# Attention's output projection: the first pair of blocks by seven block products on half of its rows, and a fixed order for the last four heads

## The chip, the cores and the metric

The kernel runs on one core of a Trainium2 chip. The metric is the device time of one launch in microseconds (us), the median of several runs. Five engines work side by side, each through its own list of instructions in order, and wait for one another by semaphores: TensorE (PE, matrix products, with its weight loads PEld), VectorE (DVE), ScalarE (ACT), GpSimd (POOL) and SyncE (SP); here SP issues nearly all loads of weights, and POOL issues loads that add into a tile that is there already.

## The reference, cut to what matters

Two decoder layers over 256 positions of width 2048. Layer 0 has recurrent mixers, layer 1 attention with 16 heads of 128; both are followed by a squared-ReLU MLP of width 8192. The part that the change touches is the end of layer 1's attention and the matrix products behind it:

```python
def dilated_attention(h, positions, w_qkv, w_o):
    qkv = (h @ w_qkv).astype(F32).reshape(bsz, seq, 3, ATTN_HEADS, HEAD_DIM)
    q = partial_rope(qkv[:, :, 0], positions) * (HEAD_DIM ** -0.5)
    k = partial_rope(qkv[:, :, 1], positions)
    v = qkv[:, :, 2]
    ...
    out = (num / den).reshape(bsz, seq, D_MODEL).astype(h.dtype)
    return out @ w_o

def squared_relu_mlp(h, w1, w2):
    return jnp.square(jax.nn.relu(h @ w1)) @ w2
...
        h = h + mix
        h = h + squared_relu_mlp(rms_norm(h, norm_mlp[layer]), mlp_w1[layer], mlp_w2[layer])
```

## The kernel before

**Precision.** Every large product is made from two-part operands: a value is split into `hi` (rounded to the format that PE takes, fp32r) and `lo` (the rest), for weights and activations alike. A product takes three passes: hi x hi, lo x hi and hi x lo. For weights, `Weights.split` (L104, L105) makes the parts: ACT casts `hi`, DVE subtracts to get `lo`. A weight tile ("slab") is 128 x 2048 float32, 1 MB, and is four sub-blocks of 128 x 512. Activations lie in `bufa` (what the projections and w1 read) and `bufb` (what w_o and w2 read): 16 blocks of 128 features, of 256 positions each, hi and lo side by side. In attention, block hd of `bufb` is the output of head hd.

**The stream of weights.** `units` lists all slabs in the order of use. `unit()` hands out the next one and, when few are left ahead, calls `fetch()`, which loads and splits another. So a split's place in the program is set by the slab that PE has begun, two to four slabs earlier, and the Tile framework's scheduler places it among the other instructions of ACT and DVE by priorities (`stream`, `urgent`). `after` and `add_manual_dep` fix an order within one engine.

**Seven products for eight.** For w1, w2 and the value part of w_qkv, the first half of the rows is taken as 2 x 2 blocks: even and odd feature blocks by two output blocks (512 columns each) of the weights, and the two halves of the positions by even and odd feature blocks of the activations. A scheme with seven products of such blocks takes the place of the usual eight. `blocks` runs it. The steps are called a, t1, t2, c, d, t3, t4, besides the plain slabs n (n2, n3, n6, n7), which have 24 matmuls each against 12 for a product step. Weights are combined on the way: s = a + t1 on DVE, the slab c is added to t1 by a load on POOL's queue, then s = s + c on DVE (L134), and a last slab is added to s by another load on POOL's queue. Activations are combined into `formh` and `formx` (`combos`, `part_forms`). Each sum lives in a PSUM bank: beta takes a, t2 and t3 in turn, alpha takes t1 and c. A bank has to be read before the next step writes it; in `second` (the w2 blocks) `to_x` does that, by adding the bank into the residual `xall`/`xres` on DVE (L769). ORDERS gives the order of the steps: for w2 and w_qkv a, t1, n7, t2, c, n6, t3, d, n2, t4, n3. `combine` (L128 to L160) holds the loads and additions of a step. For all but w1 it orders the addition s = s + c behind the split of the slab fetched at that time (`after(i, [made[u].last])`).

**The end of attention.** For each head `scores` projects q (16 + 16 matmuls, `project`), normalises and rotates it (`normed`, `rope`: L431 to L436, L869 to L872 on DVE), does the same for k, multiplies q by k on PE (L882, L883), adds the mask table (L885), takes the maximum (L889), exponentials with a running sum on ACT (L224), a reciprocal and a scaling (L891, L893), transposes the three blocks on PE (L896) and copies them out on ACT (L898). `mix` multiplies the values by these weights (L904, L905) and splits the result into `bufb` (L251 on ACT, L252 on DVE). Heads 12 to 15 run as `mix(12 + i, scores(40 + 2 * i), vg)`. Matmuls that go through `mm` or `turn` are kept in program order on PE by `chain`; those through `T.matmul` and `T.transpose` are placed by the scheduler.

**The output projection.** `out_project` takes w_o plainly, for each of four output blocks four slabs by `tokens`, `add_res` adds the sums to the residual (L624), and `to_features` transposes the result, splits it into `bufa` and, for the first two blocks, makes `formx`. The host lays w_o out beforehand, as it does the other weights. `PAIRED` is the order of feature blocks that the scheme of seven products wants, which brings the halves of the rows next to each other.

Of the kernel before, what the change touches and what calls it, by code (L numbers as in the profile page):

```python
# [41 lines left out]
def trunk_kernel(ctx, tc, x, xtok, cols, tab, masks, pos, fin, w_in, w_gate, w_out, w_qkv, w_o, w1, w2, out):  # L42
# [22 lines left out]
    units = []  # L65
    made = {}

    def plan(src, n):
        units.extend((src, i) for i in range(n))

    def plan2(src, i):
        for what, u in ORDERS[src is not w1]:
# [8 lines left out]
    for layer in range(2):  # L81
        if layer:
            for v, heads in ((0, 24), (32, 8)):
                plan2(w_qkv, v)
                units.extend((w_qkv, v + 8 + i) for i in range(heads))
            plan(w_o, 16)
        for q in range(4):
            for src in (w1, w2):
                for n in range(0, 4, 2):
                    plan2(src, layer * 64 + q * 16 + 4 * n)  # L90
    at = [0, 0]

    class Weights:
# [7 lines left out]
        def split(self, at, n):  # L101
            h, l = self.part(at, n)
            w = self.raw[:, at:at + n]
            A.copy(h, w)  # L104
            i = V.tensor_tensor(l, w, h.bitcast(F32), OP.subtract)  # L105
            self.ins = getattr(i, "ins", i)
            self.last = self.ins.name

        def part(self, at, n):
            return self.hi[:, at:at + n], self.lo[:, at:at + n]  # L110
# [12 lines left out]
            nc.sync.dma_start(r, src[i])  # L123
            made[u] = Weights(r, 1024)

    held, waiting, read = {}, [], []

    def combine(u, src, i, what, i0):  # L128
        def load(name, j, home=wraw):
            held[name] = home.tile([P, 2048], F32, name="raw" if home is wraw else name)  # L130
            nc.sync.dma_start(held[name], src[j])

        def add(to, x, y):
            return V.tensor_tensor(held[to], held[x], held[y], OP.add)  # L134
# [12 lines left out]
        if ahead == ("t2",):  # L147
            load("c", i0 + 5)
            nc.gpsimd.dma_start(held["t1"], src[i0 + 5], accum_op=OP.add)
            if src is not w1:  # L150
                make()
            i = add("s", "s", "c")
            if src is not w1:
                after(i, [made[u].last])
        if src is w1 or ahead != ("t2",):
            make(2048 if src is w1 or what != "t2" else 0)
        if src is not w1 and what == "t2":
            waiting.append(made[u])
        if what == "c":
            nc.gpsimd.dma_start(held["s"], src[i0 + 1], accum_op=OP.add)  # L160

# [33 lines left out]
    def turn(out_, in_):  # L195
        chain[:] = [after(T.transpose(out_, in_, ident), chain)]  # L196

    later, turns = [], []

    def flush(due=None):  # L200
        todo = later[:due]
# [139 lines left out]
            V.scalar_tensor_tensor(r, t, 1.5, r, op0=OP.add, op1=OP.mult)  # L341

    def tokens(src, i0, mov, kgs=(0, 1, 2, 3), by_k=False):
        ks = range(KB)
        ps = [pmm.tile([P, 512], F32, name="p") for _ in range(2)]
        for g in kgs:
            w = unit(src, i0 + g)
            order = [(j, i) for i in range(4) for j in range(2)] if by_k else \
                [(j, i) for j in range(2) for i in range(4)]
            for j, i in order:  # L350
                k = ks[4 * g + i]
                h, l = w.part(i * 512, 512)
# [297 lines left out]
    def out_project(src, gname, kgs):  # L650
        nrm = Norm()
        for n in range(4):
# [6 lines left out]
    def blocks(src, i0, n0, mov, forms, events, final):  # L659
# [21 lines left out]
        for what, u in ORDERS[src is not w1]:  # L681
            w = unit(src, None if u is None else i0 + 4 * n0 + u)
            due = len(later)
            if what != "n":
                times(bank[what], w, side[what])
                if what in events:
                    events[what](bank[what])
                if what == "t1" and waiting:
                    with stream():
                        w = waiting.pop()  # L690
                        w.split(0, 2048)
                        tc.add_manual_dep(w.ins, read[-1], NOSYNC, reason="order on one engine")
            else:
                n, g = divmod(u, 4)
                plains[n] += 1
                for j in (1, 0) if n else (0, 1):
                    times(sums[n, j], w, lambda i, j=j, g=g: plain(j, 4 * g + i))
                    if plains[n] == 2:
                        final(n, j, sums[n, j])
                flush(due)  # L700
            turn_some()

    def to_h(n, tiles):
# [58 lines left out]
        blocks(w1, i0, n0, bufa, formx, {"a": hold("y1", A.copy, 2), "t1": hold("y4", V.tensor_copy), "t2": hold("y2", A.copy),  # L762
                                             "t3": u3}, final)

    def second(i0, n0, nrm, r2, r2n, done, gains):
        def to_x(bank, j, n, r, last):
            at = slice(n * 512, n * 512 + 512)
            with urgent():
                read[:] = [after(V.scalar_tensor_tensor(xres[:, j, at], bank, r[:, j:j + 1], xres[:, j, at],  # L769
                                                        op0=OP.mult, op1=OP.add), [])]  # L770
                if nrm and last:
                    nrm.add(j, n)
# [93 lines left out]
    def rope(t):  # L866
# [5 lines left out]
        V.tensor_tensor(t[:32], a, b, OP.add)  # L872

    def scores(u0):
        p = project(w_qkv, u0, bufa)
        q = normed(p, "hz", 3)
        rope(q)
        p = project(w_qkv, u0 + 1, bufa)
        k = normed(p, "hz", 3)
        rope(k)  # L880
        ps_ = psc.tile([P, 384], F32, name="pl", bufs=2)
        T.matmul(ps_[:, :P], q[:, :P], k[:, :P], start=True, stop=True)  # L882
        T.matmul(ps_[:, P:], q[:, P:], k, start=True, stop=True)  # L883
        s = wk.tile([P, 384], F32, name="as", bufs=2)
        V.scalar_tensor_tensor(s, ps_, P ** -0.5, lnc, op0=OP.mult, op1=OP.add)  # L885
        nm = wk.tile([P, 2], F32, name="nm", bufs=2)
# [3 lines left out]
            lut(s[:, sl], s[:, sl], AF.Exp, bias=nm[:, j:j + 1], accum_out=ll[:, j:j + 1])  # L890
        V.reciprocal(ll, ll)  # L891
        for j, sl in enumerate((slice(0, P), slice(P, 384))):
            V.tensor_scalar(s[:, sl], s[:, sl], ll[:, j:j + 1], None, op0=OP.mult)  # L893
        pt = psc.tile([P, 384], F32, name="pd", bufs=1)
        for j in range(3):
            T.transpose(pt[:, j * P:j * P + P], s[:, j * P:j * P + P], ident)  # L896
        st = wk.tile([P, 384], F32, name="pT", bufs=4)
        A.copy(st, pt)  # L898
        return st

    def mix(hd, st, vg, bank="po", bufs=1):
        vs = slice((hd % 8) * P, (hd % 8) * P + P)
        po = psc.tile([P, S], F32, name=bank, bufs=bufs)
        T.matmul(po, vg[:, 0, vs], st[:, :S], start=True, stop=False, skip_group_check=True)  # L904
        T.matmul(po[:, P:], vg[:, 1, vs], st[:, S:], start=False, stop=True, skip_group_check=True)  # L905
        split_to(bufb[:, hd], po)

    with urgent():
# [139 lines left out]
def _layout(a):  # L1048
# [25 lines left out]
    def gate(w):  # L1074
# [40 lines left out]
```

## Time and profile before

| | |
|---|---|
| median of 3 runs | 2163.06 us (2162.26 to 2163.99) |
| profiled execution | 2163.68 us |
| its span, first to last instruction | 2161.4 us |
| mean granted PE clock | 0.998 |
| loaded | 485.64 MB in all, mean 225 GB/s |
| SP's loads from w (the MLP slabs) | 224 of 1 MB, 7.0 us from issue to landing |
| POOL's adding loads | 32 into t and 32 into s, 8.9 and 9.2 us |
| last q and k projections of attention done, first matmul of w_o | at 1385.70 us of the span |

How to read it: a row of a timeline has the start in us from the span's beginning, the busy time in us, the engine, the line and the operation, the tiles (out <- in), partitions x elements, and how many equal instructions in a row it stands for (x16). In brackets stands the idle time of the engine just ahead, and the work that ended it. Matmuls overlap in the pipeline, so the distance of two starts is the price of one, not its busy time. A row of windows lists busy time and count for PE, PEld, DVE, ACT and POOL, then the granted PE clock, the busy share of the DMA engines and GB/s. A row of the chain view gives the shares of the span that each engine holds on the chain of work that ended last.

### The profile page before, as it was taken

How to read it: one execution, taken by the hardware profiler on the slowest of the kernel's cores; microseconds unless marked ns; L12 is line 12 of the kernel's file. 1: busy time of each engine (PE TensorE's matmuls, PEld its weight loads, DVE VectorE, ACT ScalarE, POOL GpSimd, SP SyncE). 2: the span in 40 equal slices, each digit the busy share in tenths (PEclk: the TensorE clock that was granted, in tenths of full speed). 3: DMA queues.
4: the chain of work that ended last, by engine and by line, in shares of the span. 5: the costliest groups of instructions: out<-in, count | busy, mean ns of one | idle time of the engine just before them, and what ended most of it. 6: DMA issues, size and time to landing. Idle time of an engine off the chain costs nothing.

```text
span 2161.4 us, 27732 instructions
## 1 busy us (share of the span) xinstructions
PE 2143.4 (99%) x11020; PEld 1828.1 (85%) x11020; DVE 1787.2 (83%) x2098; ACT 1269.7 (59%) x1415; POOL 61.9 (3%) x77
## 2 busy tenths in 40 slices
PE   9999999999999999999999999999999999999998
PEld 7999998888888888888888888888888888888886
DVE  7776787688888888888988897767888988988886
ACT  7444485566466566557665545455755755755764
POOL 0000000000000000000000000000000000000000
PEclk9999999999999999999999999999999999999999
DMA  8444446577877787887785556456878778787884
GB/s 319 157 156 159 154 156 215 176 238 265 247 243 243 263 250 226 280 253 234 235 271 198 173 160 230 159 191 215 247 225 288 238 248 261 245 251 244 265 254 153
DMA packets 68736, 485.64 MB, mean 225 GB/s; under 512 B 7664, under 2 KB 8432, under 8 KB 10624
## 3 DMA queue, kind: packets, MB, share of 16 engines
q1 hardware_dynamic: 58176, 410.89, 51.5%
q0 software_dynamic: 10144, 72.39, 18.1%
q8 instruction: 86, 1.41, 0.3%
q10 hardware_dynamic: 288, 0.61, 0.1%
q14 instruction: 42, 0.34, 0.0%
HBM read 481.76 MB, written 2.10 MB: 224 GB/s over the span
## 4 chain that ended last, share of the span: by engine, by line
PE 92%; DVE 3%; ACT 2%; issue 1%; DMA 1%; SPq 0%; ACTq 0%; DVEq 0%
PE p L193 63%; PE pd L193 12%; PE po L193 12%; PE pl L196 2%; ACT hi L104 1%; DVE s L134 1%; DVE lo L105 1%; PE pl L489 1%; PE pt L193 1%; DVE xall L769 1%; DMA raw<-in_w 0%; DMA xall<-in_x 0%; PE pl L883 0%; PE po L904 0%; PE pd L896 0%
## 5 line engine op out<-in xcount | busy, mean ns | idle before, releaser
L105 DVE TENSOR_TENSOR lo<-raw,hi 128x2048 fp32r<-128x2048 f32 (+2 forms) x468 | 815.4, 1760 | 218.1 <-ACT hi L104 202.6
L104 ACT CAST hi<-raw 128x2048 fp32r<-128x2048 f32 (+2 forms) x468 | 683.7, 1484 | 508.6 <-PE p L193 273.9
L193 PE MATMUL p<-hi,bufb 128*128 128x512 f32 x1408 | 451.6, 392 | 2.4 <-DVE xall L769 1.9
L193 PE MATMUL p<-hi,bufa 128*128 128x512 f32 x1136 | 366.3, 391 | 1.3 <-ACT hi L104 1.3
L193 PE MATMUL p<-bufa,hi 128*128 128x256 f32 (+1 forms) x1792 | 365.2, 317 | 0.1
L193 PEld LDWEIGHTS p<-hi,bufb 128*128 128x128 f32 x1408 | 264.2, 188 | 62.1 <-DVE xall L769 6.7
L193 PEld LDWEIGHTS p<-bufa,hi 128*128 128x128 f32 x1792 | 294.2, 190 | 18.6 <-DVE hz L431 0.3
L193 PE MATMUL p<-lo,bufb 128*128 128x512 f32 x704 | 274.4, 390 | 0.3 <-DVE lo L105 0.3
L193 PE MATMUL p<-bufa,lo 128*128 128x256 f32 x1152 | 256.7, 287 | 0.0
L105 DVE TENSOR_TENSOR lo<-s,hi 128x2048 fp32r<-128x2048 f32 x102 | 233.3, 2287 | 28.2 <-ACT hi L104 26.0
L193 PEld LDWEIGHTS p<-hi,bufa 128*128 128x128 f32 x1136 | 213.3, 188 | 48.5 <-ACT hi L104 2.5
L104 ACT CAST hi<-s 128x2048 fp32r<-128x2048 f32 x102 | 195.1, 1913 | 100.0 <-DVE s L134 57.3
L193 PE MATMUL p<-lo,bufa 128*128 128x512 f32 x568 | 221.9, 391 | 2.1 <-DVE lo L105 2.1
L193 PEld LDWEIGHTS p<-bufa,lo 128*128 128x128 f32 x1152 | 189.8, 191 | 2.7
L193 PEld LDWEIGHTS p<-lo,bufb 128*128 128x128 f32 x704 | 132.3, 188 | 27.2 <-DVE lo L105 0.9
L193 PEld LDWEIGHTS p<-lo,bufa 128*128 128x128 f32 x568 | 106.7, 188 | 25.4 <-DVE lo L105 4.0
L193 PE MATMUL pd<-hi,bufa 128*128 128x512 f32 x288 | 95.2, 392 | 0.0
L193 PE MATMUL p<-hi,formx 128*128 128x512 f32 x288 | 94.5, 389 | 0.0
L105 DVE TENSOR_TENSOR lo<-t,hi 128x2048 fp32r<-128x2048 f32 x34 | 77.8, 2288 | 13.0 <-ACT hi L104 13.0
L193 PE MATMUL po<-hi,bufa 128*128 128x512 f32 x256 | 84.9, 393 | 0.0
L193 PE MATMUL p<-hi,formh 128*128 128x512 f32 x256 | 84.0, 389 | 0.0
L193 PE MATMUL pd<-hi,bufb 128*128 128x512 f32 x256 | 83.0, 389 | 0.0
(302 smaller groups left out, 2889.5 us busy)
## 6 DMA issues: line engine op xcount, KB each, us to landing
raw<-in_w SPq DMA_DIRECT2D x224, 1024.0 KB, 7.0
raw<-in_w_in SPq DMA_DIRECT2D x46, 1024.0 KB, 5.0
raw<-in_w_qkv SPq DMA_DIRECT2D x46, 1024.0 KB, 4.9
t<-in_w SPq DMA_DIRECT2D x32, 1024.0 KB, 7.2
t<-in_w POOLq DMA_DIRECT2D x32, 1024.0 KB, 8.9
s<-in_w POOLq DMA_DIRECT2D x32, 1024.0 KB, 9.2
raw<-in_w_out SPq DMA_DIRECT2D x16, 1024.0 KB, 4.8
raw<-in_w_o SPq DMA_DIRECT2D x16, 1024.0 KB, 4.9
```

Source lines behind the costliest of these rows:

```text
L104: A.copy(h, w)
L105: i = V.tensor_tensor(l, w, h.bitcast(F32), OP.subtract)
L134: return V.tensor_tensor(held[to], held[x], held[y], OP.add)
L193: chain[:] = [after(T.matmul(*args, **kw), chain)]
L196: chain[:] = [after(T.transpose(out_, in_, ident), chain)]
L489: T.matmul(pl[:, j], kq[:, js], halves(qp[:, js], c, True), start=True, stop=True)
L769: read[:] = [after(V.scalar_tensor_tensor(xres[:, j, at], bank, r[:, j:j + 1], xres[:, j, at], op0=OP.mult, op1=OP.add), [])]
```

## The change

- The first pair of w_o's output blocks goes through `second` and `blocks` (now with arguments for the weight, the factors and the forms), with the seven products on the half of the rows that belongs to heads 0 to 7; heads 8 to 15 stay plain. w_o gets its own entry in ORDERS: a, t1, n6, t2, c, d, n7, t3, n2, t4, n3. Its slabs are laid out in PAIRED order; `tokens` reads them so in the second pair.
- `mixed_forms` combines the outputs of heads 0 to 7 into `formx`, ahead of the last four heads.
- `scores` is cut into `turned_to` (projection and rotation), `weights_of` (scores to scaled weights) and `over_keys` (transposes and copy). The last four heads are written out in one order, all their matmuls through the chain: head hd's query projection, the mix of head hd - 2 (from head 14 on), `weigh(hd - 1)`, head hd's key projection, `over(hd - 1)`. Behind the loop stands `mix(13)`, which the loop has done already. The rest of heads 14 and 15 is put between the steps of w_o's first pair by `between`: behind t1 the mix of 14 and the scores of 15, behind t2 the transposes of 15, behind c the mix of 15.
- w_o's slab a + t1 is combined as for the other blocks; its s = s + c runs behind a and behind the last rotation; the split of n6 is ordered behind the last scaling.
- In `combine`, the order of s = s + c behind the split of the slab fetched with it is taken away for all blocks (w2 and w_qkv too): the addition is issued first, the split behind it.

```diff
-    def plan(src, n):
-        units.extend((src, i) for i in range(n))
+    order_of = lambda src: ORDERS[0 if src is w1 else 2 if src is w_o else 1]
...
-            plan(w_o, 16)
+            plan2(w_o, 0)
+            units.extend((w_o, 8 + i) for i in range(8))
...
         if ahead == ("t2",):
             load("c", i0 + 5)
             nc.gpsimd.dma_start(held["t1"], src[i0 + 5], accum_op=OP.add)
-            if src is not w1:
-                make()
-            i = add("s", "s", "c")
-            if src is not w1:
-                after(i, [made[u].last])
-        if src is w1 or ahead != ("t2",):
-            make(2048 if src is w1 or what != "t2" else 0)
+            if src is w_o:
+                between["a", 0] = lambda: after(add("s", "s", "c"), ropes[-1:])
+            else:
+                add("s", "s", "c")
+        make(2048 if src is w1 or what != "t2" else 0)
         if src is not w1 and what == "t2":
             waiting.append(made[u])
+        if src is w_o and i == i0 + 6:
+            tc.add_manual_dep(made[u].ins, scales[-1], NOSYNC, reason="order on one engine")
...
     def tokens(src, i0, mov, kgs=(0, 1, 2, 3), by_k=False):
-        ks = range(KB)
+        ks = PAIRED if src is w_o else range(KB)
...
-        beta = psc.tile([P, 512], F32, name="pt" if src is w_qkv and i0 else "po" if n0 else "pd", bufs=1)
+        beta = psc.tile([P, 512], F32, name="pt" if src is w_o or src is w_qkv and i0 else "po" if n0 else "pd", bufs=1)
...
+            between.pop((what, u), lambda: None)()
             turn_some()
...
-    def second(i0, n0, nrm, r2, r2n, done, gains):
+    def second(i0, n0, nrm, r2, r2n, done, gains=None, src=w2, forms=None):
...
-        blocks(w2, i0, n0, bufb, formh,
+        blocks(src, i0, n0, bufb, forms or formh,
...
-    for i in range(4):
-        mix(12 + i, scores(40 + 2 * i), vg)
-
-    mixers.close()
-    pair, formh = open_pairs(1)
-    nrm = out_project(w_o, "nmlp1", (0, 1, 2, 3))
+    z = both.tile([P, 2048], F32, name="s").rearrange("p (m i j c) -> p m i j c", m=4, i=2, j=2)
+
+    def mixed_forms(m):
+        zm, b = z[:, m], bufb[:, 2 * m:2 * m + 2].bitcast(F32)
+        V.tensor_tensor(zm.rearrange("p i j c -> p i (j c)"), b[..., :S], b[..., S:], OP.add)
+        a11, a21, a12, a22 = (zm[:, i, j] for i in range(2) for j in range(2))
+        combos(a22, a11, a21, a12, a11, a21, a12, a22)
+        part_forms(formx, m, 1, slice(0, 4), zm.rearrange("p i j (one c) -> p one (i j) c", one=1))
+
+
+    for m in range(4):
+        mixed_forms(m)
+    ends = {}
+
+    def last_mix():
+        nonlocal pair, formh
+        mix(15, ends[15], vg, mm=mm)
+        mixers.close()
+        pair, formh = open_pairs(1)
+
+    def weigh(hd):
+        ends[hd] = weights_of(*ends[hd], mm)
+
+    def over(hd):
+        ends[hd] = over_keys(ends[hd], turn)
+
+    for hd in range(12, 16):
+        q = turned_to(16 + 2 * hd)
+        if hd > 13:
+            mix(hd - 2, ends[hd - 2], vg, mm=mm)
+        if hd > 12:
+            weigh(hd - 1)
+        k = turned_to(17 + 2 * hd)
+        if hd > 12:
+            over(hd - 1)
+        ends[hd] = q, k
+    mix(13, ends[13], vg, mm=mm)
+    between.update({("t1", 4): lambda: (mix(14, ends[14], vg, mm=mm), weigh(15)),
+                    ("t2", 5): lambda: over(15), ("c", None): last_mix})
+    nrm = Norm()
+    second(0, 0, nrm, 1.0, -1.0, lambda n: to_features(n, "nmlp1", formx), src=w_o, forms=formx)
+    out_project(w_o, "nmlp1", (0, 1, 2, 3), (2, 3), nrm)
...
-ORDERS = (_A + (("n", 6),) + _B + (("n", 7),) + _C, _A + (("n", 7),) + _B + (("n", 6),) + _C)
+ORDERS = (_A + (("n", 6),) + _B + (("n", 7),) + _C, _A + (("n", 7),) + _B + (("n", 6),) + _C,
+          _A + (("n", 6),) + _B + (("d", 1), ("n", 7), ("t3", None), ("n", 2), ("t4", None), ("n", 3)))
...
-        "w_in": c(np.concatenate(w_in)), "w_gate": c(w_gate), "w_out": c(toks(n(a["rec_w_out"][0]))),
-        "w_qkv": c(np.concatenate(w_qkv)), "w_o": c(toks(n(a["attn_w_o"][0]))),
+        "w_qkv": c(np.concatenate(w_qkv)), "w_o": c(toks(n(a["attn_w_o"][0]), PAIRED)),
```

More of the change, by code (lines that the diff above doesn't have):

```diff
@@ L66, in trunk_kernel @@
     made = {}
-    def plan(src, n):
-        units.extend((src, i) for i in range(n))
+    order_of = lambda src: ORDERS[0 if src is w1 else 2 if src is w_o else 1]
     def plan2(src, i):
-        for what, u in ORDERS[src is not w1]:
+        for what, u in order_of(src):
             units.append((src, None if u is None else i + u, what, i))
@@ L106, in split @@
             self.ins = getattr(i, "ins", i)
-            self.last = self.ins.name
         def part(self, at, n):
@@ L124, in fetch @@
             made[u] = Weights(r, 1024)
-    held, waiting, read = {}, [], []
+    held, waiting, read, ropes, scales = {}, [], [], [], []
     def combine(u, src, i, what, i0):
@@ L196, in turn @@
         chain[:] = [after(T.transpose(out_, in_, ident), chain)]
-    later, turns = [], []
+    later, turns, between = [], [], {}
     def flush(due=None):
@@ L648, in to_features, with out_project @@
         turns.extend([-half if forms else 0, lambda half=half: work(half)] for half in range(2))
-    def out_project(src, gname, kgs):
-        nrm = Norm()
-        for n in range(4):
+    def out_project(src, gname, kgs, ns=range(4), nrm=None):
+        nrm = nrm or Norm()
+        for n in ns:
             add_res(tokens(src, 4 * n, bufb, kgs), n, nrm)
@@ L680, in blocks @@
         plains = [0, 0]
-        for what, u in ORDERS[src is not w1]:
+        for what, u in order_of(src):
             w = unit(src, None if u is None else i0 + 4 * n0 + u)
@@ L768, in to_x @@
             with urgent():
-                read[:] = [after(V.scalar_tensor_tensor(xres[:, j, at], bank, r[:, j:j + 1], xres[:, j, at],
+                r = r if isinstance(r, float) else r[:, j:j + 1]
+                read[:] = [after(V.scalar_tensor_tensor(xres[:, j, at], bank, r, xres[:, j, at],
                                                         op0=OP.mult, op1=OP.add), [])]
@@ L871, in rope, with turned_to, weights_of @@
         V.tensor_tensor(a, a, angles["sin"], OP.mult)
[L872 to L880, printed above, removed]
+        ropes.append(after(V.tensor_tensor(t[:32], a, b, OP.add), []))
+    def turned_to(u):
+        z = normed(project(w_qkv, u, bufa), "hz", 3)
+        rope(z)
+        return z
+    def weights_of(q, k, mm=T.matmul):
         ps_ = psc.tile([P, 384], F32, name="pl", bufs=2)
-        T.matmul(ps_[:, :P], q[:, :P], k[:, :P], start=True, stop=True)
-        T.matmul(ps_[:, P:], q[:, P:], k, start=True, stop=True)
+        mm(ps_[:, :P], q[:, :P], k[:, :P], start=True, stop=True)
+        mm(ps_[:, P:], q[:, P:], k, start=True, stop=True)
         s = wk.tile([P, 384], F32, name="as", bufs=2)
@@ L899, in scores, with mix @@
         return st
-    def mix(hd, st, vg, bank="po", bufs=1):
+    def scores(u0):
+        q = turned_to(u0)
+        return over_keys(weights_of(q, turned_to(u0 + 1)))
+    def mix(hd, st, vg, bank="po", bufs=1, mm=T.matmul):
         vs = slice((hd % 8) * P, (hd % 8) * P + P)
         po = psc.tile([P, S], F32, name=bank, bufs=bufs)
-        T.matmul(po, vg[:, 0, vs], st[:, :S], start=True, stop=False, skip_group_check=True)
-        T.matmul(po[:, P:], vg[:, 1, vs], st[:, S:], start=False, stop=True, skip_group_check=True)
+        mm(po, vg[:, 0, vs], st[:, :S], start=True, stop=False, skip_group_check=True)
+        mm(po[:, P:], vg[:, 1, vs], st[:, S:], start=False, stop=True, skip_group_check=True)
         split_to(bufb[:, hd], po)
```

7 lines of the change are left out of this document (5 added, 2 removed).

## The prediction

> **What bounds the kernel now.** First the page: the busy times of the engines, then the shares of the chain that ended last.
>
> ```profile
> PE 2143.4 (99%) x11020; PEld 1828.1 (85%) x11020; DVE 1787.2 (83%) x2098; ACT 1269.7 (59%) x1415; POOL 61.9 (3%) x77
> PE 92%; DVE 3%; ACT 2%; issue 1%; DMA 1%; SPq 0%; ACTq 0%; DVEq 0%
> ```
>
> TensorE is nearly always at work and carries 92% of the chain. So the time changes in two ways only: by matmuls taken away or added, and by stalls of TensorE. The price of a matmul comes from the PE timeline in the output projection; between these two rows lie 30 starts:
>
> ```profile
> 1385.94 0.40 PE L193 MATMUL p<-lo,bufb 128*128 128x512 f32 x1
> ...
> 1392.76 0.39 PE L193 MATMUL p<-lo,bufb 128*128 128x512 f32 x1
> ```
>
> 6.82 / 30 = 0.227 us each. The duration column (0.4) overlaps with the next one; starts are what counts.
>
> **Part 1: seven products for eight.** The first pair of output blocks takes 8 slabs of 24 matmuls, 192. In the changed program seven products of 12 (one sub-block by four quarters by three passes) and four plain slabs of 24 make 180. 12 x 0.227 = -2.7 us.
>
> **Part 2: one mix twice.** The loop over the last heads applies head 13's weights to its values, and the line after the loop does it again. Its price on TensorE, from the PE timeline:
>
> ```profile
> 1370.86 0.59 PE L904 MATMUL po<-pT,vg 128*128 128x256 f32 x2
> 1371.29 0.39 PE L905 MATMUL po<-pT,vg 128*128 128x128 f32 x2
> 1371.43 1.67 PE L193 MATMUL p<-bufa,lo 128*128 128x256 f32 x12
> ```
>
> 1371.43 - 1370.86 = +0.6 us. Its split on ACT and DVE (some 0.4 us each) lies beside projections and counts nothing.
>
> **Part 3: the stall behind head 15 goes.** Today the last mix is followed at once by the output-projection slab that reads it:
>
> ```profile
> 1406.67 0.38 PE L905 MATMUL po<-pT,vg 128*128 128x128 f32 x2
> 1407.51 0.50 PE L193 MATMUL p<-hi,bufb 128*128 128x512 f32 x1 [0.46 <-ACT bufb L251]
> 1407.85 0.40 PE L193 MATMUL p<-lo,bufb 128*128 128x512 f32 x1
> 1408.24 0.73 PE L193 MATMUL p<-hi,bufb 128*128 128x512 f32 x2
> ```
>
> Undisturbed, the next matmul starts 0.14 behind (1371.29 to 1371.43); here it is 0.84. The two that follow come 0.34 and 0.39 apart instead of 0.227. Lost: 0.70 + 0.11 + 0.16 = 1.0 us. In the changed order, product d, which reads heads 1, 3, 5 and 7, stands behind that mix, and the first matmul on head 15 comes 21 matmuls, 4.8 us, later: -1.0.
>
> **Part 4: the order of one addition, in all blocks of w2.** This part is not in the title. Until now s + c was ordered on DVE behind the split of the slab ahead of t2; now the rule is gone and the addition is issued first. Why that matters, PE rows first (an early n0=0 block, then the last block of the kernel), then DVE's of the early one:
>
> ```profile
> 519.71 0.39 PE L193 MATMUL p<-hi,bufb 128*128 128x512 f32 x1
> 520.27 0.50 PE L193 MATMUL p<-hi,bufb 128*128 128x512 f32 x1 [0.17 <-DVE xall L769]
> 520.60 0.39 PE L193 MATMUL p<-lo,bufb 128*128 128x512 f32 x1
> ...
> 2117.76 0.39 PE L193 MATMUL p<-hi,bufb 128*128 128x512 f32 x1
> 2118.67 0.50 PE L193 MATMUL p<-hi,bufb 128*128 128x512 f32 x1 [0.52 <-DVE xall L769]
> ```
>
> ```profile
> 514.40 2.29 DVE L105 TENSOR_TENSOR lo<-raw,hi 128x2048 fp32r<-128x2048 f32 x1 [3.02 <-ACT hi L104]
> 516.61 2.28 DVE L134 TENSOR_TENSOR s<-s,raw 128x2048 f32<-128x2048 f32 x1
> 518.81 0.74 DVE L769 SCALAR_TENSOR_TENSOR xall<-pd,nm,xall 128x512 f32<-128x512 f32 x1
> 519.47 0.74 DVE L769 SCALAR_TENSOR_TENSOR xall<-p,nm,xall 128x512 f32<-128x512 f32 x1
> ```
>
> PE waits for DVE to read t1's bank (the last row), which stands behind the addition. It loses (0.56 - 0.227) + (0.33 - 0.227) = 0.44 us; the eight n0=0 blocks run the same order, so 8 x 0.44 = 3.5. The last block loses 0.91 - 0.227 = 0.7. DVE idles 3.02 us ahead of 514.40, and the addition takes 2.2 of it, if c is there. The load of c, by the SP queue's timeline and the DMA issues of its window (the last column is us to landing):
>
> ```profile
> 502.53 0.33 SPq L131 DMA_DIRECT2D raw<-in_w  x1
> ...
> raw<-in_w SPq DMA_DIRECT2D x1, 1024.0 KB, 5.0
> ```
>
> It lands at 507.5, DVE is free from 511.4, so the addition ends at 513.6, the split starts at 514.40 as before, and the two reads start 2.2 us earlier, 517.3 instead of 519.47. PE does not need that bank before 519.93. So -4.2 us; bounds 0 (the reads slip behind other work) and -4.2.
>
> **Part 5: the chain of heads 12 to 15, first new stall.** In the changed program every matmul of these heads is chained in program order. Head 12's transposes stand right behind head 13's key projection and ahead of head 14's query projection. Today they are inside a projection; from the PE and DVE timelines:
>
> ```profile
> 1363.84 2.08 PE L193 MATMUL p<-bufa,lo 128*128 128x256 f32 x16
> ...
> 1365.99 0.27 PE L896 MATMUL pd<-tab__181,as 128*128 128x128 f32 x1
> ```
>
> ```profile
> 1362.71 0.16 DVE L891 RECIPROCAL ll<-ll 128x2 f32<-128x2 f32 x1
> 1362.79 0.41 DVE L435 TENSOR_TENSOR hz<-p,t 128x256 f32<-128x256 f32 x1
> 1363.11 0.55 DVE L893 TENSOR_SCALAR as<-as,ll 128x128 f32<-128x128 f32 x2
> ...
> 1366.01 2.36 DVE L105 TENSOR_TENSOR lo<-raw,hi 128x1024 fp32r<-128x1024 f32 x2 [0.46 <-PE p L193]
> 1368.28 0.42 DVE L435 TENSOR_TENSOR hz<-p,t 128x256 f32<-128x256 f32 x1
> ```
>
> The reciprocal and the scaling were done 2 us before the projection ended. The changed program's instruction order on DVE puts two things ahead of that reciprocal: a weight split whose buffer comes free only with the last matmul of head 13's key projection, and the new addition a + t1. Nothing is left for PE meanwhile, because the transposes block all that follows. From the point where PE could have gone on: 0.26 until the split starts (1363.84 + 16 x 0.12 = 1365.75, split at 1366.01), split 2.27, addition 2.20 (516.61 to 518.81), reciprocal 0.08, hz 0.32, first scaling 0.28, start of PE 0.06: +5.5 us. Bounds: 3.2 without the addition, 6 with full durations instead of start distances.
>
> **Part 6: second new stall.** Head 15's transposes stand between t2 and c. Ahead of its scaling, in the orders of DVE and ACT: the addition s + c, the casts of t2 and c, the exponentials, a table load, the cast of d, the split of d. Rows (ACT timeline, then two groups of the page):
>
> ```profile
> 1397.16 0.40 ACT L224 ACTIVATE as<-as,nm 128x128 f32<-128x128 f32 x1 [2.71 <-DVE nm L889]
> ...
> 1398.17 1.28 ACT L224 ACT_TABLE_LOAD   x1
> ...
> 1399.57 1.98 ACT L104 CAST hi<-raw 128x1024 fp32r<-128x1024 f32 x2
> ```
>
> ```profile
> L105 DVE TENSOR_TENSOR lo<-s,hi 128x2048 fp32r<-128x2048 f32 x102 | 233.3, 2287 | 28.2 <-ACT hi L104 26.0
> ...
> L104 ACT CAST hi<-s 128x2048 fp32r<-128x2048 f32 x102 | 195.1, 1913 | 100.0 <-DVE s L134 57.3
> ```
>
> 2.2 + 2 x 1.9 + 2.4 (1397.16 to 1399.57) + 1.9 + 2.3 + 0.3 = 12.9 us. PE has in that time head 14's mix (0.6, part 2) and head 15's scores, whose operands have the same shapes (0.6), n6 (24 x 0.227 = 5.4), t2 (2.7) and the end of t1. If the addition starts together with that mix the cover is 9.3, with all of t1 (2.7) left 12.0. Head 15's rotation, which it follows, ends late in t1, so I take 0.4 left: cover 9.7, +3.2 us; bounds 0.9 and 3.6.
>
> **Part 7: nothing.** The forms of heads 0 to 7 (4 additions and 4 subtractions on 128x512, 0.7 each like the reads above, and 16 combinations of 0.29, about 10 us) and two accumulating loads.
>
> ```profile
> 1300.00:1345.00 45.00, 45.00 (x216) 37.81 (x215) 32.66 (x32) 26.61 (x31) 0.85 (x1) 1.00 0.69 234
> ...
> 1421.15 0.29 DVE L610 TENSOR_TENSOR y<-y 128x128 f32<-128x128 f32 x1
> ```
>
> In that window (columns: PE, PEld, DVE, ACT, POOL) PE does not stall and DVE has 12 us free; without that cover it would be up to 10 us. Small waits at t2's split and head 14's transposes: +0.3 (0 to 1.1).
>
> **Part 8: the clock.** After the last matmul the granted clock falls:
>
> ```profile
> 2151.22 0.39 PE L193 MATMUL po<-hi,bufb 128*128 128x512 f32 x1
> ...
> 2154.50:2155.00 0.50, 0.00 (x0) 0.00 (x0) 0.43 (x3) 0.30 (x2) 0.00 (x0) 0.81 0.60 246
> 2155.00:2156.00 1.00, 0.00 (x0) 0.00 (x0) 0.89 (x2) 1.00 (x2) 0.00 (x0) 0.50 0.99 401
> ```
>
> 0.81 in the half microsecond means a fall at 2154.8, 3.2 us behind the last matmul's end. A wait of 5.5 us is longer. No row shows the return: lost is 0 if the fall comes later than PE's restart, 1.6 if half rate lasts as long again (3.2 us at half speed). I take the middle, +0.8; upper bound 3.2, if it lasts twice as long.
>
> [...]
>
> **The sum**, against the profiled execution (2163.68, its span 2161.4): -2.7 + 0.6 - 1.0 - 4.2 + 5.5 + 3.2 + 0.3 + 0.8 = +2.5. That execution lies 0.6 above the median of 2163.06; added to the median: 2165.6 us. The saving is real, and the chain hands it back.
>
> **Rivals.** *The clock falls twice and stays down* (slower): the second wait, 3.2 us, is as long as the fall took in the trace. If it falls there too (1.6) and the first costs 3.2 instead of 0.8: 2165.6 + 2.4 + 1.6 = 2169.6. It decides from waits of 3.2 us on. Against: the second wait is only just there.
> *The reads of w2's banks stay late* (slower): if s + c waits for c, part 4 gives nothing: 2169.8. It needs c to land over 2 us after DVE is free (513.4 in the block shown); it landed 4 us before.
> *No new stalls* (faster): if the scaling of heads 12 and 15 stays covered as it is today, parts 5, 6 and 8 fall away: 2165.6 - 9.5 = 2156.1. For it: today's reciprocal was early. Against: the split ahead of it waits for PE itself.
> *Only the first stall, at its lower bound* (3.2), with the second at 0.9 and the clock kept: 2165.6 - 2.3 - 2.3 - 0.8 = 2160.2.
>
> **How the numbers follow.** Likeliest: both stalls, near the sum, 0.64, own range 2163 to 2167.4. Clock twice 0.15, late reads 0.07, no stalls 0.06, weak stalls 0.08. A measurement of this kernel tells about 0.2% (4.3 us) from no change: bounds 2158.7 and 2167.4. Faster: no stalls and a little of the weak ones, 0.07. Slower: clock twice, most of the late reads and the upper edge of the likeliest, 0.26. Same: 0.67. The range reaches to both neighbours, 2160.0 to 2169.6.
>
> **What would show it.** A PE wait of 5 to 6 us ahead of head 12's transposes, released by DVE's scaling; one of about 3 ahead of head 15's; no wait on the t1 bank in the n0=0 blocks of w2; none on bufb in the output projection; two mixes of head 13; a window with clock below 1.00 behind the first wait. The prediction is wrong if DVE does that reciprocal ahead of the split, or if w2's blocks still wait.

## The result, and the profile after

| | before | after |
|---|---|---|
| median, 21 runs each | 2162.75 us (2162.20 to 2163.99) | 2165.95 us (2164.99 to 2169.13) |
| ratio after / before | | 1.0015 (95% interval 1.0009 to 1.0022) |
| profiled execution, its span | 2163.68, 2161.4 us | 2166.78, 2165.0 us |
| mean granted PE clock | 0.998 | 0.997 |

The changed kernel is 3.2 us slower, within 0.2%. Twelve matmuls fewer, and waits gone in the blocks of w2, were paid back by two new waits of TensorE and by its clock. The page of the changed kernel, busy times and chain (its lines are shifted by one: the matmul L193 is now L192, the addition L134 now L133, the read of the banks L769 now L770; the chained transposes stand at L195, the line of `turn`):

```profile
PE 2140.5 (99%) x11012; PEld 1831.0 (85%) x11012; DVE 1807.0 (83%) x2124; ACT 1277.0 (59%) x1415; POOL 63.6 (3%) x79
PE 95%; DVE 2%; DMA 1%; ACT 1%; issue 1%; SPq 0%; DVEq 0%
```

PE's matmuls fell by 8, the 12 saved less 4 for the second mix. Its busy time fell by 2.9 us and the span grew by 3.6, so 6.5 us are waits (and the busy time left holds some slow matmuls, below). Where PE waits, from the view of waits of PEld (us in total, times, longest), first a row of the kernel before, then one of the changed kernel:

```profile
PEld p L193 <- DVE xall L769: 6.7, 15, 0.9
```

```profile
PEld pd L195 <- DVE as L893: 8.6, 2, 5.5
```

The first row, the waits for t1's bank in w2, is gone in the changed kernel. New are two waits of a transpose for DVE's scaling. The first of them, in the timelines of PE and then of DVE:

```profile
1357.28 2.07 PE L192 MATMUL p<-bufa,lo 128*128 128x256 f32 x16
1364.65 0.95 PE L195 MATMUL pd<-tab__181,as 128*128 128x128 f32 x3 [5.30 <-DVE as L893]
1365.26 5.49 PE L192 MATMUL p<-bufa,hi 128*128 128x512 f32 x16
1370.59 1.59 PE L192 MATMUL p<-bufa,lo 128*128 128x256 f32 x12
```

```profile
1359.44 2.36 DVE L105 TENSOR_TENSOR lo<-raw,hi 128x1024 fp32r<-128x1024 f32 x2 [0.78 <-PE p L192]
1361.72 2.29 DVE L133 TENSOR_TENSOR s<-raw,t 128x2048 f32<-128x2048 f32 x1
1363.92 0.16 DVE L891 RECIPROCAL ll<-ll 128x2 f32<-128x2 f32 x1
...
1364.32 0.54 DVE L893 TENSOR_SCALAR as<-as,ll 128x128 f32<-128x128 f32 x2
```

The split waits for PE (its releaser is the last matmul of head 13's key projection), the new addition stands behind it, and only then come reciprocal and scaling. PE could have gone on at 1357.28 + 16 x 0.12 = 1359.20 (16 matmuls of the same shape took from 1351.04 to 1352.95 just before, 0.12 each) and went on at 1364.65: 5.45 us.

Behind that wait the 16 matmuls of head 14's query projection take 1370.59 - 1365.26 = 5.33 us instead of 16 x 0.227 = 3.63. The windows say why (the column behind the five engines is the granted clock):

```profile
1361.00:1362.00 1.00, 0.00 (x0) 0.00 (x0) 1.00 (x2) 0.00 (x0) 0.00 (x0) 0.93 0.00 0
1362.00:1363.00 1.00, 0.00 (x0) 0.00 (x0) 1.00 (x1) 0.00 (x0) 0.00 (x0) 0.50 0.86 123
...
1368.00:1369.00 1.00, 1.00 (x5) 0.82 (x4) 0.00 (x0) 0.00 (x0) 0.00 (x0) 0.66 1.10 229
1369.00:1370.00 1.00, 1.00 (x6) 0.84 (x5) 0.00 (x0) 0.00 (x0) 0.00 (x0) 1.00 0.98 205
```

0.93 means a fall at 1361.86, 0.66 a return at 1368.68: 6.8 us at half rate, of which PE worked from 1364.65 on, 4.0 us, and lost half, 2.0 us.

The second wait, PE and then DVE:

```profile
1407.90 0.39 PE L192 MATMUL pt<-hi,formx 128*128 128x512 f32 x1
1410.95 0.70 PE L195 MATMUL pd<-tab__181,as 128*128 128x128 f32 x3 [2.66 <-DVE as L893]
```

```profile
1406.82 0.16 DVE L891 RECIPROCAL ll<-ll 128x2 f32<-128x2 f32 x1
1408.41 2.29 DVE L105 TENSOR_TENSOR lo<-raw,hi 128x2048 fp32r<-128x2048 f32 x1 [1.44 <-ACT hi L104]
1410.62 0.54 DVE L893 TENSOR_SCALAR as<-as,ll 128x128 f32<-128x128 f32 x2
```

3.05 - 0.23 = 2.8 us. The reciprocal was done at 1406.98, a microsecond before PE needed anything; the split of d was put between it and the scaling, and had to wait for ACT first.

In w2, the same early block as in the prediction, DVE and then PE at the step onto t1's bank:

```profile
511.95 2.28 DVE L133 TENSOR_TENSOR s<-s,raw 128x2048 f32<-128x2048 f32 x1
515.07 2.29 DVE L105 TENSOR_TENSOR lo<-raw,hi 128x2048 fp32r<-128x2048 f32 x1 [0.83 <-ACT hi L104]
...
518.07 0.75 DVE L770 SCALAR_TENSOR_TENSOR xall<-p,nm,xall 128x512 f32<-128x512 f32 x1
```

```profile
520.14 0.39 PE L192 MATMUL p<-lo,bufb 128*128 128x512 f32 x1
520.37 0.62 PE L192 MATMUL p<-hi,bufb 128*128 128x512 f32 x2
520.82 0.39 PE L192 MATMUL p<-lo,bufb 128*128 128x512 f32 x1
```

The addition fills DVE's idle time, the bank is read by 518.82, 1.8 us before PE needs it (the second matmul of the row at 520.37), and the matmuls run on at 0.227. One block does pay, the last of layer 0. DVE first, then PE:

```profile
1058.10 2.29 DVE L133 TENSOR_TENSOR s<-s,raw 128x2048 f32<-128x2048 f32 x1 [1.34 <-DMA raw<-in_w]
...
1061.17 2.28 DVE L105 TENSOR_TENSOR lo<-raw,hi 128x2048 fp32r<-128x2048 f32 x1
```

```profile
1062.08 0.48 PE L192 MATMUL p<-hi,bufb 128*128 128x512 f32 x1
1063.51 0.50 PE L192 MATMUL p<-lo,bufb 128*128 128x512 f32 x1 [0.95 <-DVE lo L105]
```

There s + c waits for its slab, and the split that stands behind it is 1.43 - 0.23 = 1.2 us late for PE.

### The profile page after: what moved, and what is told of

The parts are those of the page before. It is cut to its first block, busy times and chain, and to the rows that moved or that the text cites. A ratio compares the mean times of both kernels' runs of the same rounds, so it can differ in the third digit from the quotient of the medians.

```text
span 2165.0 us, 27754 instructions
## 1 busy us (share of the span) xinstructions
PE 2140.5 (99%) x11012; PEld 1831.0 (85%) x11012; DVE 1807.0 (83%) x2124; ACT 1277.0 (59%) x1415; POOL 63.6 (3%) x79
## 4 chain that ended last, share of the span: by engine, by line
PE 95%; DVE 2%; DMA 1%; ACT 1%; issue 1%; SPq 0%; DVEq 0%
PE p L192 65%; PE pd L192 12%; PE po L192 12%; PE pl L195 2%; PE pt L192 1%; PE pl L488 1%; DVE lo L105 1%; DMA raw<-in_w_in 1%; DMA raw<-in_w 0%; ACT hi L104 0%; PE pl L883 0%; PE pd L897 0%; PE po L912 0%; PE pd L472 0%; ACT L223 0%
## 5 line engine op out<-in xcount | busy, mean ns | idle before, releaser
L192 PE MATMUL p<-hi,bufb 128*128 128x512 f32 x1336 | 426.1, 390 | 0.0
L192 PE MATMUL p<-hi,bufa 128*128 128x512 f32 x1136 | 366.5, 391 | 1.6 <-ACT hi L104 1.6
L192 PE MATMUL p<-bufa,hi 128*128 128x256 f32 (+1 forms) x1792 | 367.2, 318 | 0.1
L192 PEld LDWEIGHTS p<-bufa,hi 128*128 128x128 f32 x1792 | 295.6, 191 | 19.1 <-DVE hz L430 0.3
L192 PEld LDWEIGHTS p<-hi,bufb 128*128 128x128 f32 x1336 | 250.8, 188 | 51.7
L192 PE MATMUL p<-lo,bufb 128*128 128x512 f32 x668 | 260.0, 389 | 0.9 <-DVE lo L105 0.9
L105 DVE TENSOR_TENSOR lo<-s,hi 128x2048 fp32r<-128x2048 f32 x105 | 240.0, 2286 | 20.4 <-ACT hi L104 18.4
L192 PEld LDWEIGHTS p<-hi,bufa 128*128 128x128 f32 x1136 | 213.4, 188 | 49.1 <-ACT hi L104 2.8
L192 PE MATMUL p<-bufa,lo 128*128 128x256 f32 x1152 | 254.8, 286 | 0.0
L104 ACT CAST hi<-s 128x2048 fp32r<-128x2048 f32 x105 | 200.9, 1913 | 59.2 <-PE po L192 21.3
L192 PE MATMUL p<-lo,bufa 128*128 128x512 f32 x568 | 221.6, 390 | 1.7 <-DVE lo L105 1.7
L192 PEld LDWEIGHTS p<-bufa,lo 128*128 128x128 f32 x1152 | 189.3, 191 | 2.7
L192 PEld LDWEIGHTS p<-lo,bufb 128*128 128x128 f32 x668 | 125.5, 188 | 27.0 <-DVE lo L105 1.3
L192 PEld LDWEIGHTS p<-lo,bufa 128*128 128x128 f32 x568 | 106.8, 188 | 24.3 <-DVE lo L105 2.9
L192 PE MATMUL p<-hi,formx 128*128 128x512 f32 x304 | 100.2, 390 | 0.0
L192 PE MATMUL pd<-hi,bufa 128*128 128x512 f32 x288 | 95.3, 392 | 0.0
L192 PE MATMUL po<-hi,bufa 128*128 128x512 f32 x256 | 84.9, 393 | 0.0
L192 PE MATMUL p<-hi,formh 128*128 128x512 f32 x256 | 84.0, 389 | 0.0
L192 PE MATMUL pd<-hi,bufb 128*128 128x512 f32 x256 | 83.0, 389 | 0.0
```

The source lines that it names most:

```text
L192: chain[:] = [after(T.matmul(*args, **kw), chain)]
```

## The experiments

Each kernel was timed in turns with the kernel before on the same chip; its ratio is to that kernel. There were three series, in which the medians of before were 2162.62, 2162.55 and 2162.80 us. The first held the order alone, the split of d, the later addition and the work in the first wait; the second the old order in w2, both at once, one mix and no waits by order; the third the rest. The changed kernel itself (2165.95) was timed apart from them, against a median of before of 2162.75, so a difference of a few tenths between series says nothing.

**The order of s + c alone, in the kernel before.**

```diff
-            if src is not w1:
-                make()
-            i = add("s", "s", "c")
-            if src is not w1:
-                after(i, [made[u].last])
-        if src is w1 or ahead != ("t2",):
-            make(2048 if src is w1 or what != "t2" else 0)
+            add("s", "s", "c")
+        make(2048 if src is w1 or what != "t2" else 0)
```

> The kernel before, with one part of the change alone: s = s + c is issued ahead of the split of the slab fetched with it, in all blocks of w2 and w_qkv. Theory (the waits of TensorE for t1's bank come from that order): the eight waits of 0.44 us and the last of 0.7 go, one late slab c may cost about 1 us: about 2158.8 us, 4 below before. Rival (the reads only slip behind other work): the waits stay, 2162.8. Rival 2 (s + c now waits for c in many blocks): above 2163.

Measured: 2158.02 us (2157.50 to 2158.24), ratio 0.9978 (0.9969 to 0.9987). The waits are gone from the trace, except for one of 0.7 us in the block with the late slab. So this line, which the change's name does not speak of, is the larger part of what the change gains.

**The same order taken back in w2, in the changed kernel.** The addition is put behind the split again for w2; the rest is as changed.

> The changed kernel with s + c behind the split again, in w2 alone. Theory (that order is worth 4.1 us in the changed kernel, after one late slab c): the waits for t1's bank return in the blocks of w2, 2165.95 + 4.1 to 4.6 = 2170.1 to 2170.6 us. Rival (the gain belongs to the kernel before alone): 2166 to 2167.

Measured: 2170.36 us (2169.69 to 2170.74), ratio 1.0035 (1.0023 to 1.0048). The waits are back as they were in the kernel before:

```profile
PEld p L195 <- DVE xall L773: 6.6, 15, 0.9
```

The order is worth 4.4 us here, and 4.6 there.

**The split of d behind head 15's scaling.**

```diff
-        if src is w_o and i == i0 + 6:
+        if src is w_o and i in (i0 + 6, i0 + 1):
```

> The changed kernel, with the split of slab d ordered behind head 15's scaling on DVE, as that of n6 is. Theory (the wait ahead of head 15's transposes, 2.8 us, is the split of d standing in front of the scaling): the wait goes, 2165.95 - 2.8 = 2163.1 us. Rival (the exponentials and the table load on ACT set it): a wait of over 1.5 us stays, 2164.7 or more.

Measured: 2163.15 us (2161.40 to 2163.38), ratio 1.0001 (0.9992 to 1.0010). In its view of waits one of the two is left:

```profile
PEld pd L195 <- DVE as L893: 5.5, 1, 5.5
```

The rest of the chain (exponentials, table load) is hidden behind PE's work; what cost 2.8 us was one split in the wrong place.

**The addition a + t1 later.**

```diff
-            add("s", "a", "t1")
+            i = add("s", "a", "t1")
+            if src is w_o:
+                after(i, ropes[-1:])
+            i = units[u][1]
```

> The changed kernel, with the addition a + t1 of w_o ordered behind the rotation of head 14's key. Theory: the wait ahead of head 12's transposes falls from 5.5 to about 3.3 us (the split of head 15's query slab is left in front of the reciprocal); the addition costs up to 1.7 us of waiting at a later head. Whether the clock falls in 3.3 us is open: if it needs a longer wait (the one of 2.8 us did not bring it down) another 2.0 us come back. About 2165.4 with the clock falling, 2163.4 without, less if the wait at head 15 shrinks with the new order. Rival (the addition is not what delays the reciprocal): the wait stays at 5.5.

Measured: 2162.20 us (2161.09 to 2163.47), ratio 0.9999 (0.9990 to 1.0007). The first wait is 3.3 us, a new one of 1.7 stands ahead of head 14's transposes, and the one at head 15 is gone, because the scheduler's order moved: 2165.95 - 2.2 + 1.7 - 2.8 = 2162.7. The clock answered the open question in an unexpected way. PE row (its lines are shifted by three) and windows:

```profile
1361.27 0.70 PE L198 MATMUL pd<-tab__181,as 128*128 128x128 f32 x3 [3.10 <-DVE as L896]
```

```profile
1362.00:1363.00 1.00, 1.00 (x5) 0.77 (x5) 0.96 (x4) 0.48 (x1) 0.00 (x0) 0.79 0.73 238
1363.00:1364.00 1.00, 1.00 (x4) 0.81 (x3) 0.37 (x1) 0.00 (x0) 0.00 (x0) 0.50 1.02 434
```

It fell, at 1362.6, when PE had been at work again for 1.3 us, and returned by 1366.

**Work in the first wait.** In the loop, behind head 13's key projection:

```diff
+        if hd == 13:
+            idle = psc.tile([P, 512], F32, name="pt", bufs=1)
+            for i in range(20):
+                mm(idle, bufa[:, 0, :P], bufa[:, 1], start=True, stop=True, skip_group_check=True)
```

> The changed kernel with 20 more matmuls of 128x512, whose result nobody reads, put on TensorE between head 13's key projection and head 12's transposes, 4.5 us of work into the wait of 5.5 us. Theory (the clock falls because TensorE idles, and that costs 2.0 us behind the wait): the granted clock stays at 1.00 there, the wait is about 1 us, and the time is 2165.95 - 2.0 = 2164.0 us though more is computed. Rival (the slow matmuls behind the wait have another cause, or the wait starts with TensorE itself): 2165.95, or up to 2170.5 if the 20 matmuls push the chain.

Measured: 2165.45 us (2163.75 to 2166.64), ratio 1.0013 (1.0004 to 1.0022). The median missed the expectation by 1.5 us, though the profiled execution (2163.75) met it. So the same kernel was profiled once more:

> The kernel with the 20 matmuls in the first wait once more, one look. Nine of its eleven executions took 2165.0 to 2166.6 us, the profiled one 2163.75 with the clock at 1.00 throughout. Theory (in the others the clock falls in the second wait of 2.8 us, depending on where the wait lies against whatever counts idle time): a profiled execution near 2165.5 shows a granted clock of 0.50 for some 3.4 us after about 1407 us; one near 2163.8 shows 1.00. Rival: an execution near 2165.5 with the clock at 1.00 there, so that something else makes the difference of 1.7.

That execution took 2166.04 us. Its second wait, and the windows behind it:

```profile
1408.85 0.96 PE L195 MATMUL pd<-tab__181,as 128*128 128x128 f32 x3 [2.66 <-DVE as L893]
```

```profile
1408.00:1409.00 1.00, 0.15 (x1) 0.15 (x1) 1.00 (x4) 0.12 (x1) 0.00 (x0) 0.82 1.02 221
1409.00:1410.00 1.00, 1.00 (x4) 0.86 (x5) 1.00 (x3) 0.15 (x1) 0.00 (x0) 0.50 1.11 295
...
1412.00:1413.00 1.00, 1.00 (x5) 0.82 (x5) 0.00 (x0) 0.00 (x0) 0.00 (x0) 0.97 0.94 393
```

With the first wait filled, the clock falls in the second one, for 3.4 us (1408.64 to 1412.05). In the profile of 2163.75 it stayed up there, with the same wait:

```profile
1404.00:1412.00 8.00, 5.33 (x26) 4.11 (x25) 5.55 (x5) 4.25 (x4) 0.00 (x0) 1.00 0.95 276
```

The fall is not the whole of the 2.3 us between the two profiles. The last matmul ahead of the wait starts at 1405.80 in the slower one and at 1404.81 in the other, so 1.0 us was there already (1.3 at the 81st matmul, some 24 us into the kernel); the fall accounts for 1.3.

**Both at once:** the 20 matmuls, and the split of d behind the scaling.

> The changed kernel with both: the 20 matmuls nobody reads in the first wait, and the split of d behind head 15's scaling. No wait longer than about 1 us is left. Theory (the clock costs 2 us; with the fill alone it fell in the second wait in most executions instead, which is why the median of that run is 1.7 above its profiled execution): the median is 2 below that of the split of d alone, 2163.15 - 2.1 = 2161.0 us, and the clock is 1.00 between 1350 and 1420 us. Rival (the fill buys 0.5 as in the medians so far, and the clock is not what costs): 2162.6.

Measured: 2160.90 us (2160.28 to 2161.53), ratio 0.9992 (0.9983 to 1.0001), in the window 1340 to 1420:

```profile
1340.00:1420.00 80.00, 79.26 (x419) 68.07 (x419) 65.59 (x116) 39.76 (x59) 1.72 (x2) 1.00 0.56 180
```

Against the split of d alone (2163.15) only the clock behind the first wait differs, since the wait for DVE is as long as before (the 20 matmuls fill most of the 5.5 us). So 4.5 us of useless work made the kernel 2.25 us faster, by the medians.

**One mix of head 13.** The line behind the loop is left out.

> The changed kernel without the second mix of head 13. Theory (its price is its time on TensorE, 0.57 us, but it stood in the cover of head 15's transposes): TensorE's wait there grows from 2.8 to about 3.3 us, so the time falls by 0.1 to 0.2 only, 2165.8 us. Rival (plain price): the wait stays at 2.8 and the time falls by 0.6, 2165.4. The wait in the trace tells them apart, the times hardly do.

Measured: 2166.99 us (2164.46 to 2168.49), ratio 1.0019 (1.0010 to 1.0027). Slower by its median than with the mix, though the intervals overlap. The trace shows more than the theory had. PE row, and windows:

```profile
1410.18 0.88 PE L195 MATMUL pd<-tab__181,as 128*128 128x128 f32 x3 [3.21 <-DVE as L893]
```

```profile
1408.00:1409.00 1.00, 0.00 (x0) 0.00 (x0) 1.00 (x1) 1.00 (x1) 0.00 (x0) 0.97 1.10 229
1409.00:1410.00 1.00, 0.00 (x0) 0.00 (x0) 1.00 (x3) 0.31 (x1) 0.00 (x0) 0.50 0.90 188
...
1415.00:1416.00 1.00, 1.00 (x4) 0.77 (x4) 0.00 (x0) 0.00 (x0) 0.00 (x0) 0.62 0.98 418
```

The wait grew by half a microsecond, as expected, and here the clock fell in it as well, for 6.8 us. The eleven executions lie in two groups, four at 2164.5 to 2164.9 and seven at 2166.8 to 2168.5; that the second fall parts them was seen in one profile (2168.49) and is inferred for the rest. In that profile PE worked at half rate from 1410.18 to 1415.76 and lost 2.8 us, and the groups lie 1.9 us or more apart.

**No waits, by order alone.** The changed kernel with one mix, a + t1 behind head 14's key rotation (as above), d's split behind head 15's scaling, and

```diff
+            if behind:
+                after(c, exps[-1:])
+                after(i, scales[-1:])
...
+            for n in scales[-1:] + (ropes[-1:] if i == i0 + 6 else []):
+                tc.add_manual_dep(made[u].ins, n, NOSYNC, reason="order on one engine")
...
+        behind[:] = [1] if hd > 13 else []
...
-    mix(13, ends[13], vg, mm=mm)
+    behind.clear()
```

where c and i are a slab's cast and its split, and exps holds the exponentials.

> The changed kernel with the waits taken away by order alone: a + t1 behind the rotation of head 14's key; from head 14 on the cast and split of a slab behind the exponentials and scalings of the head before; n6's split behind head 15's rotation, too; the split of d behind head 15's scaling; the second mix of head 13 left out. Theory: no wait over 1 us from 1340 to 1420, the clock stays up; 2162.6 (before) - 4.6 (order in w2, measured alone) - 2.7 (12 matmuls) - 1.0 (wait at head 15 of before) + some 2 us of small waits at new places = 2156.3 us. Rival (the 10 us of added DVE work come out as waits elsewhere, so that the product scheme is worth nothing): 2158.0, the time of the order alone, or more.

Measured: 2156.64 us (2156.38 to 2158.05), ratio 0.9973 (0.9963 to 0.9983); once more in the last series 2156.38, ratio 0.9971 (0.9959 to 0.9982).

> The kernel with the waits taken away by order once more, on the same chip as the two above, so that the step of 1 us to the exception can be seen: 2156.6 us.

The window of the first of the two runs:

```profile
1340.00:1420.00 80.00, 78.96 (x414) 66.86 (x413) 69.69 (x116) 40.92 (x60) 1.72 (x2) 1.00 0.58 188
```

PE is at work for 78.96 of 80 us, with the clock at 1.00. The time is 9.3 us below the changed kernel by the medians, with the same products, save the second mix.

**The late slab.** The same kernel, and then the kernel before, with the new order of s + c everywhere but in the last block of w2 in layer 0 (i0 = 56).

> The kernel with the waits taken away by order, and in one block of w2 alone, the last of layer 0, s + c behind the split as before the change. Theory (there s + c stands ahead of a slab c that lands late, and holds up the split behind it: 1.0 us of TensorE's waiting): that wait goes, 2156.6 - 1.0 = 2155.6 us. Rival (the old order brings its own wait for t1's bank back in that block): 2156.6.

> The kernel before with the order of s + c changed in all blocks but that one, and nothing else. Theory: 2158.0 - 0.8 = 2157.2 us. Beside the run with the waits taken away and the same exception it shows what the seven products on half of the rows are worth once no order costs anything: 2.7 + 1.0 less some 2.3 of small waits, 1.4 us. Rival (worth nothing): the two are equal.

Measured: 2155.81 us (2155.52 to 2156.69), ratio 0.9968 (0.9956 to 0.9981), and 2157.02 us (2156.56 to 2158.24), ratio 0.9974 (0.9963 to 0.9984). The first is the fastest version of the study. It is 0.6 below its neighbour in the series (2156.38), whose trace has 0.8 us of waiting in that block; the ranges of the two overlap, so the times alone do not show that step, but the wait is gone from the trace. Between the two versions with the exception lies what the seven products are worth with every order mended: 1.2 us by the medians, near the 1.4 expected, but the intervals overlap.

## Why the prediction was right, point by point

The time, its direction within 0.2%, and the mechanism came out as forecast (2165.6 against 2165.95). That the number is so near is partly luck. The forecast rise was 2.5 us on a median of before of 2163.06, from three runs; with 21 runs that median was 2162.75, and the rise 3.2. And inside the sum, errors offset one another, as the steps show:

- **Part 1, twelve matmuls, -2.7; part 3, the wait at head 15, -1.0:** both as worked out. The matmuls are gone from PE (the count above), and there is no wait on bufb in the list of waits. The runs with the orders mended put what is left of their 3.7 us at 1.2; the trace of the fastest version has 2.7 us of new small waits between 1385 and 1440 us.
- **Part 2, the second mix, +0.6:** the price was right and the entry was wrong. The mix stands on PE ahead of the second wait and is cover for it. Taking it away saved nothing; the wait grew from 2.8 to 3.4 us. Added work ahead of a wait has to be entered against that wait, not in the sum.
- **Part 4, -4.2:** measured -4.6 alone in the kernel before and 4.4 the other way in the changed one. The bound of "over 2 us after DVE is free" for a late slab was read from one block and does not hold in all: in the last block of layer 0, where DVE has other work queued, a slab 1.34 us late cost PE 1.2 us. So this rival came true in one block.
- **Part 5, +5.5:** measured 5.45, in the order and by the instructions named.
- **Part 6, +3.2:** measured 2.8. The chain on DVE and ACT took 12.8 us (1398.15, where the addition s + c starts, to 1410.95) and the cover was 10.0, against 12.9 and 9.7. That the split of d alone makes it was shown by moving it.
- **Part 7, 0 and +0.3:** the forms of heads 0 to 7 cost nothing: no row of the view of waits of PEld names them. The small waits were not found behind t2's split or head 14's transposes in the changed kernel.
- **Part 8, the clock, +0.8:** too small, the term that was mis-sized. The profile shows 2.0 us, and the pair of runs with and without the fill, both with the split of d moved, 2.25 by the medians. It was taken from one fall at the end of the kernel, and two things were missing: the fall came 2.5 us behind PE's end, not 3.2, and half rate went on for 6.8 us, not 3.2. This term was 1.2 too small, parts 4, 6 and 7 together came out 1.1 below their forecast, so the parts as measured, -2.7 + 0.6 - 1.0 - 4.6 + 5.45 + 2.8 + 2.0, again add up to about 2.5. The two profiled executions lie 3.1 apart, but 0.65 of that is there at the 81st matmul (start at 23.75 and 24.40 us), ahead of all that was changed. Why the medians lie 3.2 apart and not 2.5 stays open.

The rival with two falls of the clock was no fiction: seen in the kernel with one mix, and the likely reason for the long upper tail of the changed kernel (up to 2169.13, predicted 2169.6), which no profile of such an execution confirms.

## What to carry to other kernels

A step written out in a fixed order on one engine is only as good as the order of its partners on the others: put each instruction that releases the fixed chain ahead of all work on its engine that waits for the same chain, or that nobody needs yet. A wait of TensorE can cost more than its length, since the clock may fall with it (here 2.0 us on top of 5.5), and it can be that work ahead of a wait is free and taking it away is dear (here the second mix, 0.6 us: without it the wait grew from 2.8 to 3.4 us and the clock fell in it in the one profile taken, and the ratio was 1.0019 in place of 1.0015, with intervals that overlap). And a change should be taken apart before it is judged: here one line of order, in another part of the kernel, gained 4.6 us, and two orders on DVE lost more than that (5.45 and 2.8 us).

## What the runs showed of the hardware that was not expected

The length of a wait is counted between starts, as above; the idle time ahead of the fall from the end of PE's last matmul.

| wait of PE | idle ahead of the fall | fall, counted from PE's return | half rate |
|---|---|---|---|
| changed kernel, first, 5.5 us | 2.5 us | 2.8 us before | 6.8 us |
| split of d, first, 5.5 us | 4.1 us | 1.2 us before | 6.8 us |
| one mix, first, 5.5 us | 2.6 us | 2.8 us before | 6.8 us |
| addition later, first, 3.3 us | 3.1 us | 1.3 us behind | about 3.4 us |
| fill, second profile, second, 2.8 us | 2.4 us | 0.2 us before | 3.4 us |
| one mix, second, 3.4 us | 2.0 us | 1.2 us before | 6.8 us |
| fill, first profile, second, 2.8 us | | none | |
| changed kernel, second, 2.8 us | | none | |

A wait of 2.8 us may or may not bring the clock down; the same kernel shows both, in the two profiles of the fill. The fall does not follow PE's stop by a fixed time: while PE stood still it came 2.0 to 4.1 us behind the end of the last matmul, 2.3 us behind the very last one of the changed kernel (2154.86 to 2157.16), and in one row when PE had been at work again for 1.3 us. And half rate lasted 3.4 us or twice that: 6.8 where the wait still went on for over a microsecond behind the fall, 3.4 where PE was back within 0.2 us or already at work.

Some distances between changes of the clock, as measured, lie near whole multiples of one length: in the changed kernel 6.83 us from fall to return (2 x 3.414) and 788.48 us from there to the fall behind its last matmul (1368.68 to 2157.16, 231 x 3.413), and in the kernel with one mix 47.79 us between the two falls (1361.15 and 1408.94, 14 x 3.414). What sets the place of a fall was not shown, and no run was made to find it. So it stays open why a wait of 2.8 us brought the clock down in one execution of the fill and not in the other.
